# A diffusion-transformer layer on one core: the first feed-forward's way down by half products, and two conditioning vectors computed elsewhere

## The chip, the cores and the metric

The kernel runs on 1 core of one Trainium2 chip. The metric is the time of one execution on the device in microseconds (us). Three runs of the kernel before took 2833.11, 2833.44 and 2836.21 us; the median is 2833.44 us.

The engines are called as in the profile: PE (TensorE, matmuls), PEld (its weight loads), DVE (VectorE), ACT (ScalarE), POOL (GpSimd) and SP (SyncE, which issues the DMAs here). SBUF is the on-chip working memory, PSUM the memory into which PE writes.

## The reference, cut to what matters

One layer with two groups of tokens, 1024 latent and 128 context tokens, which the kernel handles together as T = 1152 columns (D = 1024 features, D_FF = 2816):

```python
def swiglu(h, w1, w3, w2):
    return (jax.nn.silu(h @ w1) * (h @ w3)) @ w2

def trunk_layer(x, mod, cache, lb, norm_g, ffn1, ffn2, mixer_w):
    m = [mod[:, i][:, None, :] for i in range(N_MOD)]
    x = x + 0.5 * m[2] * swiglu(modulate(x, norm_g[0], m[0], m[1]), *ffn1)
    mix, ctx = token_mixer(modulate(x, norm_g[1], m[3], m[4]), cache, lb, *mixer_w)
    x = x + m[5] * mix
    x = x + 0.5 * m[8] * swiglu(modulate(x, norm_g[2], m[6], m[7]), *ffn2)
    return x, ctx
...
        mod_p = (jax.nn.silu(c_ctx) @ w_ada[l] + b_ada[l]).reshape(1, N_MOD, D_MODEL)
        mod_s = (jax.nn.silu(c) @ w_ada[l] + b_ada[l]).reshape(c.shape[0], N_MOD, D_MODEL)
```

The "way up" of a feed-forward is `silu(h @ w1) * (h @ w3)`, its "way down" the product with `w2` (2816 x 1024) and the addition to x. The nine conditioning vectors `m[0]` to `m[8]` are rows of a matrix product of SiLU(c) (latent) and SiLU(c_ctx) (context) with `w_ada`; vectors 6 and 7 are first needed in the second feed-forward's norm.

## The kernel before, in words

Features lie on the 128 partitions, tokens along the free axis. Features come in 8 tiles (KT), hidden rows of a feed-forward in 22 tiles (NF), called rows 0 to 21 here. Each float32 product is made of three matmuls of a high and a low part: `wh*xh`, `wh*xl`, `wl*xh` (`mm3`, L535 to L542). The split into parts takes a copy on ACT and a subtraction on DVE or POOL.

The stages in order: first feed-forward up and down, mixer projections with the recurrence (`hgrn`), attention (`attn`, `heads`), merge, second feed-forward up and down, final norm. `ffn_fast` (L2181) runs a feed-forward; `l` is 0 for the first, 1 for the second.

**Half products.** A product of 2 x 2 blocks can be had with seven block products instead of eight, if sums of the blocks are formed before and after. `PRODUCTS` lists the order of the seven. The way up uses this in both feed-forwards (`fast_block`, L1882) after four (l = 0) or three (l = 1) plain rows: per row 7 products x 2 pairs of token quarters x 4 feature tiles x 3 matmuls of 288 columns = 168. Weights are made up to six products ahead by `fast_ops`: POOL forms sums (L1872), ACT the high part (L1876), DVE the low part (L1877).

**The second way down** uses it too. Pairs of rows 3 to 18 are taken in three groups of 2, 3 and 3 pairs (`GROUPS`). During the way up, `pair_sums` (L1933; DVE, L1939 to L1942) makes sums of the hidden rows and stores them in DRAM (`xd`), and `pair_weights` (L1948; POOL, L1965 to L1968) makes sums of quarters of `w2` and stores them (`wsum`). Then `down_sweep` (L2074) takes, per group and per pair of output tiles, seven products of 288 columns; `down_ops` supplies the split weights, `down_xs` the split hidden sums, and DVE adds to x (L2090). The remaining rows go plainly (`down_group`, `down_last`).

**The first way down** goes plainly, all of it: nine groups of two rows (`down_group`) and a last one of four (`down_last`), each over 8 output tiles and 3 chunks of 384 columns, with DVE adding each result to x (L569).

**Conditioning vectors.** Vectors 0 and 1 are made at the start by PE. The rest are made on DVE by `ada_sum` (L362): a transposed tile of `w_ada` times a broadcast row, 512 columns, with a running sum (L393), 32 such operations a vector, as two halves x 8 tiles x 2 rows. Vectors 2 to 5 are made in the first way up, 6 and 7 in the first way down (`self.bg`; one step after every third block of PE's work), 8 in the second way up. Their loads (256 KB each) go by SP's queue into two half tiles in turn; each load waits until DVE is done with the half tile.

**Order of the work.** A scheduler orders the instructions of each engine ahead of time, by the order in which the program emits them and by when their data and buffers should be ready; each engine then runs its list in order. The program weaves side work in by hand: generators (`ada`, `sums`, `xg`, `pre`, ...) advance by `next` at fixed points of the main loops. Large tiles (27 of them, tag `T`, `self.tt`) and smaller ones are shared by all stages. In `hgrn` a head has three chunks; PE's products of the scan stand among projection matmuls (`work`), which fill PE while DVE, POOL and ACT work on the chain of a chunk. In `heads` a head has two blocks of 9 key tiles; row maxima of the next block (`rowmax`: PE L1549, DVE L1550, two PSUM tiles), queries, keys and values of the next heads run beside.

Of the kernel before, what the change touches and what calls it, by code (L numbers as in the profile page):

```python
# [19 lines left out]
P = 128  # L20
# [13 lines left out]
H = 8  # L34
# [11 lines left out]
GROUPS = (3, 2), (7, 3), (13, 3)  # L46
# [47 lines left out]
class Trunk:  # L94
# [3 lines left out]
    def run(self):  # L98
        self.part, self.mode, self.chunks, self.bg = {}, "ffn1", ORDER, iter(())
        nc, tc, a = self.nc, self.tc, self.a  # L100
        with ExitStack() as st:
# [5 lines left out]
            self.xs = self.dp.tile([KT, P, T], F32, name="xs")  # L107
            self.modt = self.cp.tile([P, 9, KT, 2], F32, name="modt")
# [253 lines left out]
    def ada_sum(self, ms, cb, w2, small):  # L362
# [14 lines left out]
        for n, (h, i, k) in enumerate(units):  # L377
            if not i and not k:
                cs = [cb() if cb else self.half("cb")[:, :HD] for _ in range(2)]
                row = [self.half("row")[:, :HD] for _ in range(2)] if cb else cs  # L380
                for s in range(2):
                    nc.sync.dma_start(row[s], a["cr"][s : s + 1, ts(h, HD)].to_broadcast([P, HD]))
                if not n:
                    load(0)
                for s in range(2):
                    nc.scalar.activation(cs[s], row[s], AF.Silu)
                yield
# [14 lines left out]
            yield  # L402

# [452 lines left out]
    def hgrn(self):  # L856
# [77 lines left out]
        for p in range(H * NCH + 1):  # L934
# [31 lines left out]
        for i, _ in enumerate(work):  # L966
            if i % 2 == 0 and todo:
# [3 lines left out]
        for n, _ in enumerate(self.proj_gate(19, 3, pairs[3])):  # L971
            if n == 0:
                self.group()

# [266 lines left out]
    def heads(self, qn, ck, ckc, KT_, ktc, rope, w0, sums):  # L1241
# [37 lines left out]
        self.pend, self.mo = [], [None] * 8  # L1279
        pre = self.preload()  # L1280
        for h in range(H):
# [8 lines left out]
            for j in range(2):  # L1290
                rm = rowmax(h, 1) if not j else iter(()) if last else rowmax(h + 1, 0)
                sd = weave(side[j])
                for t, _ in enumerate(self.block(h, j, Q[h % 2], kset(h), vset(h))):
                    next(rm, None)
                    if t in SIDE:
# [3 lines left out]
                for _ in chain(rm, sd):  # L1299
                    pass  # L1300
        for _ in pre:
# [646 lines left out]
    def pair_weights(self, w2):  # L1948

        nc, pin = self.nc, self.tc.keep_in_program_order  # L1950
        self.wsum = self.dp.tile([sum(n for _, n in GROUPS), P, KT // 2, 4, P], F32, name="wsum")
        n = sum(n for _, n in GROUPS)
        for j in range(n):
            f = GROUPS[0][0] + 2 * j
            for m in range(KT // 2 if j < n - GROUPS[-1][1] else 1):
# [18 lines left out]
    def down_ops(self, w2):  # L1974

        nc = self.nc
        units = [(j, n, m) for j, n in enumerate(n for _, n in GROUPS) for m in range(KT // 2)]
# [5 lines left out]
        def load(u, key):  # L1983
# [3 lines left out]
            j, f = sum(v for _, v in GROUPS[:g]), GROUPS[g][0]  # L1987
            own = g == len(GROUPS) - 1 and m > 0
# [28 lines left out]
        for u, (g, n, m) in enumerate(units):  # L2017
            load(u + 1, 6)
            load(u + 1, 2)
            if g == len(GROUPS) - 1 and m:  # L2020
# [26 lines left out]
    def down_xs(self, g, X):  # L2047

        nc = self.nc
        j0 = sum(n for _, n in GROUPS[:g])  # L2050
        units = [(i, k) for i in PRODUCTS for k in range(GROUPS[g][1])]
# [22 lines left out]
    def down_sweep(self, g, m, X, ops, made, gm, S, after):  # L2074

        nc = self.nc
        n = GROUPS[g][1]
        first, last = g == 0, g == len(GROUPS) - 1
# [45 lines left out]
    def down_fast(self, w2, X, xg, ops, made, load_x, load_h, split_h, gm, nxt):  # L2124

        S = [self.tt(F32, "su")[:, :T].rearrange("p (m n) -> p m n", m=4) for _ in range(2)]
        rest = [2, *range(PLAIN[1] + 16, NF)]
        pend, ws = [], []
        self.folds = []
        for g, (f, n) in enumerate(GROUPS):  # L2130
            new = {} if g else X
            last = g == len(GROUPS) - 1
# [48 lines left out]
    def ffn_fast(self, l, gm, nxt):  # L2181
# [5 lines left out]
        self.puts, self.ticks, self.roles = [], 0, {}  # L2187
# [39 lines left out]
        spare = partial(self.tt, F32R) if l == 0 else partial(self.wide, dt=F32R)  # L2227
# [6 lines left out]
        def load_h(f):  # L2234
            if l and f < 2:
# [8 lines left out]
        def split_h(f, raw):  # L2244
            new = partial(self.tt, F32R) if f in (16, 17) and not l else split
# [11 lines left out]
        def load_w2(f):  # L2257
            return self.load_w(w2[f], 1, D, home=spare if f % 2 else None)

        sums = self.pair_weights(w2) if l else iter(())  # L2260
        dops, dmade, X = (self.down_ops(w2) if l else None), [], {}
        xg = self.down_xs(0, X) if l else None
        for f in range(plain, NF):
# [3 lines left out]
            for n in range(7):  # L2267
# [14 lines left out]
                if f == NF - 1 and l:  # L2282
# [4 lines left out]
                    for _ in range(GROUPS[0][1]):  # L2287
# [3 lines left out]
                    for k in ((0, 4), (), (), (), (1, 5), (2, 6), (3, 7))[n]:  # L2291
                        self.x[k] = self.tt(F32, f"x{k}")
                        if k % 4 < 3:
                            nc.sync.dma_start(self.x[k][:, :T], self.xs[k])
                elif f == NF - 1:
                    if n == 2:
                        raws = [load_h(0), load_h(1)]
                    elif n == 3:
                        ws.append(load_w2(0))
                        pend.append(split_h(*raws[0]))  # L2300
                    elif n == 4:
                        pend.append(split_h(*raws[1]))
                    elif n == 5:
                        ws.append(load_w2(1))
                        self.x = [load_x(0), load_x(1)]
# [3 lines left out]
        if not l:  # L2309
            self.x += [load_x(k) for k in range(2, KT)]  # L2310
        if l == 0:
            self.mixer_consts()
            self.bg = self.ada_sum((6, 7), lambda: self.bank("up", "cb", D // 2), partial(self.tt, F32), self.slim)
        if l:
            self.down_fast(w2, X, xg, dops, dmade, load_x, load_h, split_h, gm, nxt)
            return
        for f in range(2, NF):
            pend.append(split_h(*load_h(f)))
            if f % 2 and f < NF - 1:
                fs, hs = zip(*pend[:2])  # L2320
                self.down_group(w2, fs, hs, gm, ws or [load_w2(v) for v in fs])
                pend, ws = pend[2:], None
        for _ in self.bg:
            pass
        fs, hs = zip(*pend)
# [124 lines left out]
```

## Time and profile before

| | us |
|---|---|
| median of three runs | 2833.44 |
| the profiled execution, whole | 2831.82 |
| its span (first to last instruction) | 2830.0 |
| mean granted TensorE clock | 0.995 of full |
| PE idle in the recurrence (818 to 1420) | 17.0 |
| PE idle in attention's heads (1540 to 1860) | 10.1 |
| DVE busy in the first way down (534 to 818) | 215.97 |

Times of lines are from the start of the span. A line of a group of instructions reads: line, engine, operation, out<-in by the program's names, out<-in (partitions x elements, type), count | busy time, mean ns of one | idle time of the engine just before them and what ended most of it. A line by stage reads: from:to, length, then for each engine its busy time and in brackets the count of its instructions, the granted clock, the mean busy share of the 16 DMA engines and the GB/s that they moved. PE's matmuls are pipelined, so one lasts longer than the step from one start to the next.

### The profile page before, as it was taken

The page shows a single profiled execution, that of the slowest core. Times are in us where ns is not written, and L with a number is a line of the kernel's source. Part 1 is how long each engine was busy: PE and PEld are TensorE (multiplying, and loading weights), DVE is VectorE, ACT ScalarE, POOL GpSimd, SP SyncE. Part 2 cuts the span into 40 slices and gives each one's busy share as a digit, 9 for nine tenths or more (in the row PEclk, how much of TensorE's full clock was granted, in tenths as well). Part 3 has the DMA queues.
Part 4 walks back from the last instruction along what each step waited for, and adds up shares of the span by engine and source line. Part 5 has one row for each costly group of instructions (what it writes and reads, how often), then busy time and mean ns, then how long its engine had stood idle before and what let it go on. Part 6 is the DMA issues. An engine that isn't in the chain of part 4 may idle for free. (4 is left out here: it accounts for less than half of the span.)

```text
span 2830.0 us, 55726 instructions
## 1 busy us (share of the span) xinstructions
PE 2763.6 (98%) x21222; PEld 2633.5 (93%) x21222; DVE 2037.8 (72%) x4464; ACT 1302.9 (46%) x2696; POOL 926.4 (33%) x980
## 2 busy tenths in 40 slices
PE   8999999999999999999999999999999999999998
PEld 7999999999999998889998778689999999999997
DVE  7867777677678787877356777766766765568875
ACT  6533332321176676666436777741552322234332
POOL 0233232444222222222244444420414443423451
PEclk9999999999999999999999999999999999999999
DMA  6743443753121111112512001263454444358521
GB/s 261 228 130 118 130 125 118 260 180 117 57 82 57 45 63 38 66 41 84 192 60 98 19 15 30 84 232 104 154 171 130 145 156 134 116 164 253 164 85 67
DMA packets 219578, 337.64 MB, mean 119 GB/s; under 512 B 23664, under 2 KB 141360, under 8 KB 219312
## 3 DMA queue, kind: packets, MB, share of 16 engines
q1 hardware_dynamic: 219312, 334.10, 36.0%
q8 instruction: 167, 2.74, 0.4%
q14 instruction: 99, 0.81, 0.1%
HBM read 248.47 MB, written 85.54 MB: 118 GB/s over the span
## 5 line engine op out<-in xcount | busy, mean ns | idle before, releaser
L1902 PE MATMUL b<-xo,wo 128*128 128x288 f32 x3552 | 482.9, 295 | 0.0
L1902 PEld LDWEIGHTS b<-xo,wo 128*128 128x128 f32 x3552 | 474.8, 188 | 0.0
L1902 PE MATMUL b<-bh,wo 128*128 128x288 f32 x1776 | 366.0, 295 | 0.0
L539 PE MATMUL mm<-xh,wh 128*128 128x384 f32 x936 | 327.2, 350 | 5.5 <-DVE q L767 4.3
L541 PE MATMUL mm<-xh,wl 128*128 128x384 f32 x936 | 317.2, 339 | 0.0
L540 PE MATMUL mm<-xl,wh 128*128 128x384 f32 x936 | 316.6, 338 | 0.0
L1902 PEld LDWEIGHTS b<-bh,wo 128*128 128x128 f32 x1776 | 288.7, 188 | 0.0
L569 DVE SCALAR_TENSOR_TENSOR x<-dn,modt,x 128x256 f32<-128x256 f32 (+4 forms) x472 | 225.6, 499 | 83.8 <-PE dn L541 81.8
L1902 PE MATMUL b<-bl,wo 128*128 128x288 f32 x888 | 261.7, 295 | 0.0
L1876 ACT CAST wo<-raw 128x512 fp32r<-128x512 f32 x185 | 114.8, 621 | 221.1 <-issue 88.1
L539 PEld LDWEIGHTS mm<-xh,wh 128*128 128x128 f32 x936 | 176.4, 188 | 12.9 <-DVE q L767 5.5
L2103 PE MATMUL d<-xd,wd 128*128 128x288 f32 x1344 | 181.7, 297 | 5.0 <-DVE x L2090 3.0
L2103 PEld LDWEIGHTS d<-xd,wd 128*128 128x128 f32 x1344 | 180.0, 190 | 6.5 <-issue 4.4
L1877 DVE TENSOR_TENSOR wo<-raw,wo 128x512 fp32r<-128x512 f32 x185 | 127.4, 689 | 79.1 <-ACT wo L1876 76.5
L540 PEld LDWEIGHTS mm<-xl,wh 128*128 128x128 f32 x936 | 176.7, 189 | 0.9
L541 PEld LDWEIGHTS mm<-xh,wl 128*128 128x128 f32 x936 | 177.0, 189 | 0.0
L1599 POOL TENSOR_TENSOR ehl<-e,ehl 128x512 fp32r<-128x512 f32 x93 | 123.9, 1337 | 154.6 <-ACT ehl L1597 83.6
L393 DVE SCALAR_TENSOR_TENSOR junk<-wada,cb 128x512 bf16<-128x512 f32 x224 | 163.9, 732 | 5.5 <-DMA wada<-in_w_aT 4.6
L1902 PEld LDWEIGHTS b<-bl,wo 128*128 128x128 f32 x888 | 167.5, 189 | 0.0
L1872 POOL TENSOR_TENSOR ws<-raw 128x256 f32<-128x256 f32 x74 | 64.5, 892 | 283.1 <-DMA raw<-in_w 254.3
L539 PE MATMUL ps<-bh,wh 128*128 128x288 f32 (+1 forms) x448 | 135.7, 303 | 3.2 <-ACT bh L532 1.9
L1877 DVE TENSOR_TENSOR wo<-ws,wo 128x512 fp32r<-128x512 f32 x74 | 69.6, 940 | 92.4 <-ACT wo L1876 91.9
(477 smaller groups left out, 7163.9 us busy)
## 6 DMA issues: line engine op xcount, KB each, us to landing
raw<-in_w SPq DMA_DIRECT2D x148, 256.0 KB, 3.5
wada<-in_w_aT SPq DMA_DIRECT2D x112, 256.0 KB, 3.1
raw<-in_w SPq DMA_DIRECT2D x42, 512.0 KB, 3.8
raw<-in_w_in SPq DMA_DIRECT2D x41, 512.0 KB, 3.5
xr<-xd SPq DMA_DIRECT2D x56, 288.0 KB, 3.8
hr<-hs SPq DMA_DIRECT2D x26, 576.0 KB, 5.7
hb<-hd SPq DMA_DIRECT2D x44, 288.0 KB, 3.8
hs<-et SPq DMA_DIRECT2D x84, 144.0 KB, 2.3
```

What stands on the lines that cost most here:

```text
L393: nc.vector.scalar_tensor_tensor(junk, ws[n % 2], 1.0, cs[s], ALU.mult, ALU.mult, accum_out=o)
L539: pin(nc.tensor.matmul(ps, wh, xh, start=start and i == 0, stop=False))
L540: pin(nc.tensor.matmul(ps, wh, xl, start=False, stop=False))
L541: self.last_mm = nc.tensor.matmul(ps, wl, xh, start=False, stop=stop and i == n - 1)
L569: nc.vector.scalar_tensor_tensor(self.x[m][:, a:b], ps[:, a - lo : b - lo], self.modt[:, gm, m, s : s + 1], self.x[m][:, a:b], ALU.mult, A ...
L1599: eng.tensor_sub(el, e, eh)
L1872: nc.gpsimd.tensor_tensor(o[:, c], x[:, c], y[:, c], op)
L1876: nc.scalar.copy(wh, src[i])
L1877: nc.vector.tensor_sub(wl, src[i], wh)
L1902: nc.tensor.matmul(ps, w[:, k], x[:, k, :QW], start=first, stop=last, skip_group_check=home != i)
L2103: nc.tensor.matmul(ps, w[:, k], xv, start=start, stop=stop, skip_group_check=home != i)
```

## The change

- The first way down goes by half products too, by the code of the second: pairs of rows 4 to 19 in groups of 2, 3 and 3. `GROUPS` has an entry for each feed-forward, and `self.groups` takes its place in the functions. Rows 0 to 3, 20 and 21 stay plain (0 and 1 as one group, the other four in `down_last`). `pair_sums`, `pair_weights` and the first steps of `down_ops` and `down_xs` now run in the first way up too.
- The background sum of vectors 6 and 7 in the first way down is gone. A new function `ada_late` makes one vector by the same 32 operations. Vector 6 is made in `hgrn` from the last head's first chunk on, one operation at each slot; vector 7 in `heads`, three operations per block.
- `ada_late` loads the rows SiLU(c), SiLU(c_ctx) from DRAM (`crow`), where `ada_sum` stores them in the first way up.
- `mixer_consts` and the loads of x stand where the second feed-forward has its own.

```diff
-GROUPS = (3, 2), (7, 3), (13, 3)
+GROUPS = ((4, 2), (8, 3), (14, 3)), ((3, 2), (7, 3), (13, 3))
...
+                    if self.mode == "ffn1":
+                        nc.sync.dma_start(self.crow[h, s : s + 1], cs[s][0:1])
...
+    def ada_late(self, m):
...
+        wt = self.tt(F32, "wada")
+        ws = [wt[:, ts(v, HD)] for v in range(2)]
+        cs = []
+        for h in range(2):
+            t = self.tt(F32, "cb")
+            cs.append([t[:, ts(s, HD)] for s in range(2)])
+            for s in range(2):
+                nc.sync.dma_start(cs[h][s], self.crow[h, s : s + 1].to_broadcast([P, HD]))
...
+        for n, (h, k) in enumerate(units):
+            if n + 1 < len(units):
+                load(n + 1)
+            for s in range(2):
+                o = acc[:, h, k, s : s + 1]
+                self.tc.keep_in_program_order(
+                    nc.vector.scalar_tensor_tensor(junk, ws[n % 2], 1.0, cs[h][s], ALU.mult, ALU.mult, accum_out=o)
+                )
+                yield
...
+            if p == H * NCH - 3:
+                ada = self.ada_late(6)
...
                     next(work, None)
                     next(pre, None)
+                    if p > H * NCH - 4:
+                        next(ada, None)
...
+        ada = self.ada_late(7)
...
                     next(rm, None)
+                    if t % 3 == 1:
+                        next(ada, None)
...
-        rest = [2, *range(PLAIN[1] + 16, NF)]
+        plain = self.groups[0][0]
+        rest = [*range(2, plain), *range(plain + 16, NF)]
...
-        if l:
-            self.xd = self.dp.tile([sum(n for _, n in GROUPS), P, 7, 2, QW], F32, name="xd")
-            self.roles = {f + v: (j, v % 2) for j, f in enumerate(range(GROUPS[0][0], PLAIN[1] + 16, 2)) for v in range(2)}
+        self.xd = self.dp.tile([sum(n for _, n in self.groups), P, 7, 2, QW], F32, name=f"xd{l}")
+        self.roles = {f + v: (j, v % 2) for j, f in enumerate(range(plain, plain + 16, 2)) for v in range(2)}
...
-        sums = self.pair_weights(w2) if l else iter(())
-        dops, dmade, X = (self.down_ops(w2) if l else None), [], {}
-        xg = self.down_xs(0, X) if l else None
+        sums = self.pair_weights(w2)
+        dops, dmade, X = self.down_ops(w2), [], {}
+        xg = self.down_xs(0, X)
...
-            self.bg = self.ada_sum((6, 7), lambda: self.bank("up", "cb", D // 2), partial(self.tt, F32), self.slim)
-        if l:
-            self.down_fast(w2, X, xg, dops, dmade, load_x, load_h, split_h, gm, nxt)
-            return
-        for f in range(2, NF):
-            pend.append(split_h(*load_h(f)))
-            if f % 2 and f < NF - 1:
-                fs, hs = zip(*pend[:2])
-                self.down_group(w2, fs, hs, gm, ws or [load_w2(v) for v in fs])
-                pend, ws = pend[2:], None
-        for _ in self.bg:
-            pass
-        fs, hs = zip(*pend)
-        self.down_last(w2, fs, hs, gm, nxt)
+        self.down_fast(w2, X, xg, dops, dmade, load_x, load_h, split_h, gm, nxt)
```

More of the change, by code (lines that the diff above doesn't have):

```diff
@@ L1986, in load @@
             g, n, m = units[u]
-            j, f = sum(v for _, v in GROUPS[:g]), GROUPS[g][0]
-            own = g == len(GROUPS) - 1 and m > 0
+            j, f = sum(v for _, v in self.groups[:g]), self.groups[g][0]
+            own = g == len(self.groups) - 1 and m > 0
             part = lambda t, h: t[:, : h * n * P].rearrange("p (h k d) -> p h k d", h=h, k=n)
@@ L2049, in down_xs @@
         nc = self.nc
[L2050 to L2051 removed]
+        j0 = sum(n for _, n in self.groups[:g])
+        units = [(i, k) for i in PRODUCTS for k in range(self.groups[g][1])]
         raws = []
@@ L2244, in split_h @@
         def split_h(f, raw):
-            new = partial(self.tt, F32R) if f in (16, 17) and not l else split
+            new = partial(self.tt, F32R) if f < 2 else split
             hh, hl = new(name="hh")[:, :T], new(name="hl")[:, :T]
```

67 lines of the change are left out of this document (36 added, 31 removed).

## The prediction, made before the changed kernel ran

> **What bounds the kernel now.** I read the page first, then the busy times by stage, then single tiles for the spacing of the matmuls, then the groups of DVE and POOL in the stages that the change touches.
>
> ```profile
> span 2830.0 us, 55726 instructions
> PE 2763.6 (98%) x21222; PEld 2633.5 (93%) x21222; DVE 2037.8 (72%) x4464; ACT 1302.9 (46%) x2696; POOL 926.4 (33%) x980
> ```
>
> TensorE is busy all along, so a stage is as long as its matmuls need, plus what they wait. The stages, with the count of instructions behind each engine's busy time:
>
> ```profile
> core 0: us, PE busy (x) PEld busy (x) DVE busy (x) ACT busy (x) POOL busy (x), PEclk, DMA share, GB/s
> 133.00:534.00 401.00, 401.00 (x3026) 401.00 (x3025) 289.33 (x646) 126.12 (x245) 128.38 (x145) 1.00 0.41 132
> ...
> 2133.00:2551.40 418.40, 418.40 (x3157) 418.40 (x3156) 268.91 (x532) 126.27 (x256) 163.73 (x238) 1.00 0.44 142
> 2551.40:2738.00 186.60, 181.60 (x1347) 180.08 (x1347) 158.23 (x306) 77.67 (x150) 78.94 (x50) 0.99 0.57 177
> ```
>
> They are the first way up by half products, the second way up, and the second way down, which already runs by half products (the first, plain, follows below). Matmuls overlap, so the mean of one (about 0.3 us) is no price; the spacing is. Both ways up have PE without a gap: 401.00 / 3026 = 0.1325 us for a 288-column matmul. The second way down needs 186.60 / 1347 = 0.1385 us for the same form, so 0.006 x 1347 = 8.1 us of it are lost.
>
> For the plain way down, its first matmul, the first of the stage behind it, and two matmuls that stand 56 apart in the timeline:
>
> ```profile
> L539 PE MATMUL dn<-hh,wh x360: 279/338/692, 534.2 to 2817.8; 128*128 128x384 f32 x156, 128*128 128x512 f32 x12, 128*128 128x256 f32 x12
> ```
> ```profile
> L539 PE MATMUL mm<-xh,fh x24: 332/338/525, 814.8 to 854.9; 128*128 128x384 f32 x24
> ```
> ```profile
> 559.75 0.34 PE L540 MATMUL dn<-hl,wxh 128*128 128x384 f32 x1
> 569.52 0.34 PE L539 MATMUL dn<-hh,wh 128*128 128x384 f32 x1
> ```
>
> The stage takes 814.8 - 534.2 = 280.6 us. Its spacing is 9.77 / 56 = 0.1745 us for 384 columns. By the code it has 22 rows x 8 outputs x 3 chunks x 3 products = 1584 matmuls, 276.4 us; 4.2 us are waits and the norm's own matmuls.
>
> **The change, part by part.**
>
> *The first way down.* Eight pairs of rows (4 to 19) go by seven products instead of eight: 8 x 4 x 7 x 2 x 3 = 1344 matmuls of 288 columns. Rows 0 to 3, 20 and 21 stay plain: 6 x 8 x 3 x 3 = 432 of 384. Without stalls that is 1344 x 0.1325 + 432 x 0.1745 + 4.2 = 257.7 us, 22.9 less. But the same code in the second way down did not run at 0.1325. What held it there:
>
> ```profile
> L2103 PE MATMUL d<-xd,wd 128*128 128x288 f32 x1344 | 181.7, 297 | 5.0 <-DVE x L2090 3.0
> ```
> ```profile
> 2670.00:2690.00 20.00, 18.01 (x125) 17.80 (x124) 19.31 (x38) 7.42 (x15) 13.31 (x10) 0.91 0.56 167
> ```
>
> PE waited 5.0 us there, mostly for DVE, which is busy for 158.23 of 186.60 us (85%). The worst wait, 2.0 us near 2678, is followed by a lower granted clock (0.91 over 20 us, so 0.09 x 20 = 1.8 us more). Splits, product counts, group sizes (2, 3, 3) and transfers of the new stage are those of this one, and the two moved vectors no longer run in it. So I take 0.1385: 186.1 + 75.4 + 4.2 = 265.7 us, **14.9 less**. Bounds: 22.9 less, and 0 if DVE holds it for as long as it lasts now.
>
> The Trainium skill ("TensorE: Matmul & The Clock Gate", Part 1) has the clock halve only after an idle window of about 3.4 us and asks for no gap over about 3 us. By that a 2.0 us wait would cost itself alone, and the gain would be 16.7; the row differs, and I keep the row.
>
> *The first way up gets the sums.* It keeps its 128 conditioning products and gains the pair sums, the quarter and weight sums and the first splits for the way down. From the second way up, where such sums stand now (DVE, then POOL), and the first way up as it is (DVE, then POOL):
>
> ```profile
> L1942 DVE TENSOR_TENSOR hp<-et 128x288 f32<-128x288 f32 x16 | 7.3, 454 | 0.3
> ...
> L2068 DVE TENSOR_TENSOR xd<-xr,xd 128x576 fp32r<-128x576 f32 x6 | 7.0, 1174 | 3.7 <-ACT xd L2067 3.7
> ```
> ```profile
> L1872 POOL TENSOR_TENSOR raw<-raw,ws 128x256 f32<-128x256 f32 x36 | 25.8, 737 | 81.7 <-DVE wo L1877 58.8 <-issue 22.8
> L1966 POOL TENSOR_TENSOR wq<-wq 128x128 f32<-128x128 f32 x22 | 14.9, 679 | 1.2
> ...
> L1968 POOL TENSOR_TENSOR wq<-wq 128x128 f32<-128x128 f32 x22 | 11.2, 509 | 0.0
> ```
> ```profile
> L393 DVE SCALAR_TENSOR_TENSOR junk<-wada,cb 128x512 bf16<-128x512 f32 x128 | 95.8, 748 | 3.0 <-DMA wada<-in_w_aT 2.3
> L1877 DVE TENSOR_TENSOR wo<-raw,wo 128x512 fp32r<-128x512 f32 x89 | 61.0, 686 | 41.6 <-ACT wo L1876 40.3
> L1877 DVE TENSOR_TENSOR wo<-ws,wo 128x512 fp32r<-128x512 f32 x36 | 34.0, 945 | 37.8 <-ACT wo L1876 37.3
> ...
> L1906 DVE TENSOR_TENSOR et<-b,et 128x288 f32<-128x288 f32 x36 | 16.4, 457 | 9.1 <-PE b L1902 9.1
> ```
> ```profile
> L1872 POOL TENSOR_TENSOR ws<-ws,raw 128x256 f32<-128x256 f32 x36 | 32.8, 931 | 0.0
> ```
>
> DVE: four groups of pair sums like the one shown, 4 x 7.3, and 7.0 for the splits are 36 us more, 289.3 + 36 = 325 of 401 us (81%). POOL: four groups on quarters of weights, from 14.9 down to 11.2, about 52 us more, 180 (45%). At 72% (now) and 64% (second way up) of DVE, PE lost nothing; at 85%, in the second way down, 8.1 of 186.6 us (4.3%). So the bounds are 0 and 4.3% x 401 = 17 us. I take **1 us**, near the two ways up: weights are split up to six ahead of their use and each is good for 24 matmuls (6 x 24 x 0.1325 = 19 us), in the way down for only 12 or 18. A gain I exclude, since PE has no gap to close.
>
> *Vector 6 at the recurrence's end.* Thirty-two products of the kind that run in the first way down now, and DVE there from the last head's first chunk (the copy at 1309.75) on:
>
> ```profile
> L393 DVE SCALAR_TENSOR_TENSOR junk<-wada,cb 128x512 bf16<-128x512 f32 x64 | 43.4, 677 | 1.0 <-DMA wada<-in_w_aT 1.0
> ...
> L393 DVE DVE_READ_ACCUMULATOR junk<-wada,cb 128x1 f32 x64 | 5.3, 82 | 0.0
> ```
> ```profile
> 1309.75 0.42 DVE L1075 COPY_PREDICATED A<-mask,lv 128x96 f32<-128x96 uint8 x2
> ```
> ```profile
> 1300.00:1325.00 25.00, 25.00 (x301) 23.54 (x301) 24.27 (x51) 12.78 (x33) 9.06 (x11) 1.00 0.20 70
> 1325.00:1350.00 25.00, 25.00 (x359) 23.28 (x358) 13.11 (x40) 14.36 (x43) 4.53 (x7) 1.00 0.29 101
> 1350.00:1375.00 25.00, 25.00 (x237) 23.68 (x236) 8.40 (x19) 10.51 (x25) 3.19 (x5) 1.00 0.41 140
> 1375.00:1400.00 25.00, 25.00 (x169) 23.56 (x167) 6.50 (x15) 12.69 (x19) 3.21 (x2) 1.00 0.79 287
> ```
>
> One costs (43.4 + 5.3) / 64 = 0.76 us, 32 cost 24 us, and DVE has 12 + 17 + 18 us free after 1325. Only the first eight, 6 us, fall where it is full. Bounds 0 and 6; I take **1**, as PE has gate matmuls in store there (25.00 of 25.00 busy). Behind each waiting load in SP's queue stand the gates' stores and the weights for the next stage:
>
> ```profile
> SPq L374 <- DVE junk L393: 229.6, 81, 5.9
> ```
>
> SP waited 2.8 us on average for such a load, 5.9 at most. Those stores and loads have 25 us and more until their use, so I price this at nothing; without that cover it would be 16 x 2.8 = 45 us on SP, some of it late weights at 1400. A vector also brings 16 loads and four broadcasts of 256 KB, 5 MB, into a DMA share of 0.20 to 0.41; at the 287 GB/s of the last row that is 18 us of transfer, over more than 50 us. Taking 64 products out of the way down (49 us of DVE) brings nothing by itself, as PE lost at most 4.2 us there.
>
> *Vector 7 in attention*, three products per block, so in the first eleven of 16 blocks. A block takes 320 / 16 = 20 us. Blocks with queries and row maxima (the first half of a head) and without alternate:
>
> ```profile
> 1540.00:1860.00 320.00, 309.92 (x1451) 243.12 (x1449) 235.91 (x437) 245.96 (x466) 147.78 (x120) 1.00 0.13 37
> ```
> ```profile
> 1620.00:1640.00 20.00, 19.94 (x95) 16.11 (x94) 16.66 (x32) 14.81 (x28) 11.55 (x10) 1.00 0.03 7
> 1640.00:1660.00 20.00, 19.94 (x97) 15.81 (x96) 13.69 (x28) 16.58 (x35) 8.38 (x7) 1.00 0.10 26
> ...
> 1800.00:1820.00 20.00, 17.82 (x83) 13.42 (x83) 19.08 (x37) 14.08 (x28) 10.24 (x8) 1.00 0.15 41
> ```
>
> Three products add 2.3 to 2.5 us (0.677 or 0.748, and 0.08 for the sum's read): 16.6 becomes 19.1 of 20 in five such halves (heads 1 to 5), 13.7 becomes 16.2 in the others. The one stretch that has 19.08 now shows PE idle for 2.18 us instead of 0.06. So the upper bound is 5 x 2.1 = 11 us, the lower 0. I take **5**, since the stretch at 1800 also brings in the next stage's tiles. Here PE waits behind row maxima: DVE frees the two PSUM tiles that PE's next row-maximum matmul needs, and everything behind it on PE waits too. On SP the weights of the next heads stand behind the vector's loads, but those come 7 us apart and find their half tile free; of the 27 large tiles 25 are held by then, so the second pair of broadcasts waits until the first pair's tile is free, once, within the bounds above.
>
> The four small stores of the conditioning rows are nothing beside 334 MB. **Sum:** -14.9 + 1 + 1 + 5 = **-7.9 us**. The profiled execution took 2831.82 us (span 2830.0), 1.6 under the median of 2833.44. From the median: **2825.5 us**.
>
> **The rivals.**
>
> *A: attention takes back what the way down gives.* For it: 19.1 of 20 us on DVE, a level at which PE loses 2 us per 20. Against: the other half of each head can absorb. At 11 us the sum is -1.9: 2831.5 us, no change.
>
> *B: DVE and POOL hold up the first way up, and the kernel gets slower.* Operations with both inputs in SBUF wait for POOL: the split behind a POOL sum takes 945 ns, the one without 686, while one that reads PSUM (457) does not differ. Busy time that needs this path would be 325 - 5 x 16.4 (five groups that read PSUM) = 243 on DVE plus 180 on POOL, 423 of 401 us; about 9 us on DVE (36 x 0.26) and some 14 on POOL (two groups, 36 x (931 - 737) ns each) are waiting counted as work, so 400: just full, where it is 289 - 82 + 128 - 23 = 312 now. In-order queues do not fill it without gaps. If it decides, the stage grows by 17 (the bound above) to 23 us, say 20: -14.9 + 20 + 1 + 5 = +11: 2844.5 us. It makes the kernel slower by over 0.2% from 15 us on. The Trainium skill ("SBUF — State Buffer", SBUF: two separate sides) calls the shared port pair an exclusive lock that blocks the loser for the whole instruction. The trace agrees by 945 against 686.
>
> *C: no stalls in the way down*, as they hang on a few collisions (5.0 us of waits): -22.9 + 7 = -15.9: 2817.5 us.
>
> *D: fewer matmuls, but not sooner.* The second way down moves the most of the stages above, 177 GB/s at a DMA share of 0.57. If the new stage waits for its transfers as much as it has fewer columns to do, the gain is gone: -14.9 + 14.9 + 7 = +7: 2840.5 us. Against: the waits of the second way down are put down to DVE, not to a DMA.
>
> **How the numbers follow.** Forecast 0.50, A 0.20, B 0.15, C 0.10, D 0.05. A measurement tells about 0.2%, 5.7 us. The forecast's own range is 2819 to 2831, of which some four fifths lie under 2827.8; with C that makes faster 0.53. A and the rest of the forecast make no change 0.29; B and half of D, slower 0.18. The range runs from 2815 (C with small stalls) to 2846 (B).
>
> **What would show it.** PE without a gap from 133 to 534 with DVE near 325 us; 1344 matmuls on the first way down's tiles at 0.138 us, the stage some 15 us shorter; PE busy 25.00 in each 25 us from 1300 to 1400; attention up to 5 us longer with PE waiting for row maxima. It is wrong if the first way up has PE waiting for split weights or PSUM tiles, or if attention grows by over 10 us, or if the way down stays over 275 us.

## The result and the profile after

The changed kernel takes 2880.97 us (median of 4 runs, 2877.97 to 2884.28) beside 2833.28 us of the kernel before (4 runs); the ratio is 1.0167, with an interval of [1.0152, 1.0183]. It is slower by 48 us, where 8 us less were forecast. The profiled execution took 2883.85 us. First the page of after, then its stages; the columns are those of the stage table in the prediction.

```profile
span 2882.0 us, 57099 instructions
PE 2770.9 (96%) x21414; PEld 2629.6 (91%) x21414; DVE 2112.3 (73%) x4587; ACT 1333.5 (46%) x2816; POOL 973.6 (34%) x1089
```
```profile
133.80:563.40 429.60, 412.28 (x3027) 408.53 (x3026) 313.95 (x717) 118.57 (x255) 180.91 (x238) 0.98 0.54 169
563.40:754.20 190.80, 182.44 (x1345) 178.94 (x1345) 161.89 (x314) 77.47 (x152) 77.83 (x51) 1.00 0.56 177
754.20:831.60 77.40, 77.40 (x438) 76.56 (x438) 51.45 (x105) 33.14 (x62) 23.55 (x16) 1.00 0.29 101
831.60:1454.10 622.50, 598.33 (x6568) 558.50 (x6567) 488.38 (x1231) 394.02 (x949) 152.34 (x230) 0.99 0.24 81
...
1560.90:1911.70 350.80, 328.71 (x1466) 256.96 (x1466) 264.73 (x507) 249.09 (x471) 151.82 (x121) 0.96 0.17 51
```

They are the first way up, the first way down by half products, its plain rest, the recurrence, and attention's heads. The same stages of before, but for the way up (401.00 us, in the prediction):

```profile
534.20:814.80 280.60, 279.30 (x1590) 277.63 (x1589) 212.57 (x498) 72.30 (x102) 107.83 (x49) 1.00 0.41 142
814.80:1430.20 615.40, 598.37 (x6568) 559.36 (x6567) 463.76 (x1165) 393.40 (x949) 151.52 (x230) 0.99 0.22 73
...
1536.90:1860.60 323.70, 313.62 (x1468) 245.91 (x1467) 237.93 (x440) 248.79 (x471) 149.38 (x121) 1.00 0.13 39
```

| stage | before | after | difference | forecast |
|---|---|---|---|---|
| first way up | 401.0 | 429.6 | +28.6 | +1 (0 to 17) |
| first way down | 280.6 | 268.2 | -12.4 | -14.9 |
| recurrence | 615.4 | 622.5 | +7.1 | +1 (0 to 6) |
| heads | 323.7 | 350.8 | +27.1 | +5 (0 to 11) |

These make +50.4 of the 52.0 us between the two profiled executions. The way down brought what it should; three stages that only took over side work gave it back five times.

**First way up.** PE idled 429.60 - 412.28 = 17.3 us; of the other 11 us, some 9 are the lower granted clock (0.02 x 429.6). DVE is busy for 314 of 430 us (73%), so it isn't full. Its waits tell more. The row answers to the L393 row of before, where 3.0 us stood in the last column (line numbers move between the kernels: L1925 and L1927 below are L1872 of before). Then come SP's longest waits in this stage, each with its total, its count and the longest one:

```profile
L396 DVE SCALAR_TENSOR_TENSOR junk<-wada,cb 128x512 bf16<-128x512 f32 x128 | 94.1, 735 | 41.0 <-DMA wada<-in_w_aT 40.6
```
```profile
SPq L2023 <- POOL wq L2020: 67.8, 18, 8.3
SPq L1907 <- DVE wo L1930: 57.7, 24, 5.3
SPq L1843 <- DVE et L1994: 49.3, 15, 5.6
```

One such place, as SP, DVE and PE saw it (start, duration, and in brackets the wait before):

```profile
321.45 0.33 SPq L2023 DMA_DIRECT2D wsum<-wq  x1
321.88 1.40 SPq L375 DMA_DIRECT2D wada<-in_w_aT  x1
323.37 0.38 SPq L2024 DMA_DIRECT2D wsum<-wq  x1
323.85 0.37 SPq L375 DMA_DIRECT2D wada<-in_w_aT  x1
```
```profile
325.95 0.69 DVE L396 SCALAR_TENSOR_TENSOR junk<-wada,cb 128x512 bf16<-128x512 f32 x1 [4.84 <-DMA wada<-in_w_aT]
326.57 0.08 DVE L396 DVE_READ_ACCUMULATOR junk<-wada,cb 128x1 f32 x1
326.57 0.45 DVE L1963 TENSOR_TENSOR et<-b,et 128x288 f32<-128x288 f32 x1
```
```profile
327.08 0.61 PE L1955 MATMUL b<-bh,wo 128*128 128x288 f32 x1 [3.80 <-DVE et L1963]
```

SP had issued nothing since 312.77: it waited 8.3 us at the store of a quarter sum (L2023), until POOL had made that sum. A conditioning load stands behind this store in SP's queue. Its product stands at the head of DVE's queue and waits 4.84 us for it. Behind the product stands the addition that frees a PSUM tile, and PE waits 3.80 us for that.

**Heads.** Vector 7's products did not run three to a block. SP's queue shows the broadcast rows loaded at once, and the vector's first weights 200 us later; the stretches of 20 us show what followed:

```profile
1560.67 0.80 SPq L420 DMA_DIRECT2D cb<-crow  x2
...
1761.42 0.81 SPq L425 DMA_DIRECT2D wada<-in_w_aT  x2
```
```profile
1741.00:1761.00 20.00, 19.96 (x97) 15.73 (x97) 15.79 (x31) 16.31 (x32) 8.88 (x8) 1.00 0.03 7
...
1781.00:1801.00 20.00, 12.74 (x38) 10.18 (x37) 18.55 (x44) 4.60 (x9) 4.75 (x4) 0.71 0.34 112
```

All 32 products run from 1764 to 1817 us, nearly every second operation of DVE there (32 of 68), and PE falls to 12.74 of 20 us at a clock of 0.71. The vector wants 28 large tiles with what attention holds (25, and one for weights and two for rows); there are 27. The weights' tile was given the place of a key tile (the low half of the first), whose last reader is a score matmul of head 4.

### The profile page after: what moved, and what is told of

Its sections match the earlier page's. It is cut to its first block, busy times and chain, and to the rows that moved or that the text cites. A ratio compares the mean times of both kernels' runs of the same rounds, so it can differ in the third digit from the quotient of the medians.

```text
span 2882.0 us, 57099 instructions
## 1 busy us (share of the span) xinstructions
PE 2770.9 (96%) x21414; PEld 2629.6 (91%) x21414; DVE 2112.3 (73%) x4587; ACT 1333.5 (46%) x2816; POOL 973.6 (34%) x1089
## 5 line engine op out<-in xcount | busy, mean ns | idle before, releaser
L1955 PE MATMUL b<-bh,wo 128*128 128x288 f32 x1776 | 375.5, 300 | 16.6 <-DVE et L1963 11.7
L2156 PE MATMUL d<-xd,wd 128*128 128x288 f32 x2688 | 364.7, 297 | 13.2 <-DVE x L2143 8.5
L2156 PEld LDWEIGHTS d<-xd,wd 128*128 128x128 f32 x2688 | 359.3, 189 | 18.4 <-ACT wd L2094 6.2
L579 PE MATMUL mm<-xh,wh 128*128 128x384 f32 x936 | 327.1, 350 | 10.5 <-DVE sg L881 4.7
L1955 PEld LDWEIGHTS b<-bh,wo 128*128 128x128 f32 x1776 | 294.9, 192 | 20.1 <-DVE et L1963 12.5
L2121 POOL TENSOR_TENSOR xd<-xr,xd 128x576 fp32r<-128x576 f32 x70 | 111.9, 1617 | 179.4 <-ACT xd L2120 177.8
L1929 ACT CAST wo<-ws 128x512 fp32r<-128x512 f32 x74 | 45.7, 618 | 244.2 <-POOL ws L1925 224.1
L2143 DVE SCALAR_TENSOR_TENSOR x<-d,modt,x 128x288 f32<-128x288 f32 (+2 forms) x324 | 137.7, 462 | 23.6 <-PE d L2156 20.8
L396 DVE SCALAR_TENSOR_TENSOR junk<-wada,cb 128x512 bf16<-128x512 f32 x160 | 118.9, 743 | 43.1 <-DMA wada<-in_w_aT 42.6
```

The source lines that it names most:

```text
L396: nc.vector.scalar_tensor_tensor(junk, ws[n % 2], 1.0, cs[s], ALU.mult, ALU.mult, accum_out=o)
L579: pin(nc.tensor.matmul(ps, wh, xh, start=start and i == 0, stop=False))
L1929: nc.scalar.copy(wh, src[i])
L1955: nc.tensor.matmul(ps, w[:, k], x[:, k, :QW], start=first, stop=last, skip_group_check=home != i)
L2121: (nc.vector if k == 1 else nc.gpsimd).tensor_sub(lo, raw, hi)
L2143: nc.vector.scalar_tensor_tensor(xv, src[:, v], self.modt[:, gm, mi, s : s + 1], xv, ALU.mult, ALU.add)
```

## The experiments

Theory: (1) in the first way up, loads stand late in SP's in-order queue behind stores that wait for other engines, and the operations that wait for these loads hold up DVE's and POOL's in-order queues; (2) in attention, the missing tile bunches the products; (3) in the recurrence, either of the two. The main rival is time: DVE, POOL and their shared path simply have too much to do. All stage lengths below are from first matmul to first matmul; a stage whose code is the same in two runs differs by up to 4.4 us (the first way up 427.3 to 431.7; the recurrence, unchanged in twelve of them, 619.1 to 621.5, beside 622.5 in after). The first way down, whose own work none of the experiments changes, takes 262.9 to 270.3 us. e1 to e13 are one execution each, so stage lengths are compared, not totals. e1, e6 and e13 leave out most loads of the vectors' weights, so they compute other vectors; they show times only.

### e1 and e2: the conditioning loads

e1, then e2 (`nw` is the count of half tiles, four):

```diff
-            if n + 1 < len(units):
+            if n + 1 < (len(units) if len(ms) == 1 else 2):
```
```diff
-        w2 = w2("wada")
-        ws = [w2[:, :HD], w2[:, HD : 2 * HD]]
+        tiles = [w2("wada") for _ in range(2 if len(ms) == 4 else 1)]
+        ws = [t[:, ts(v, HD)] for t in tiles for v in range(2)]
...
-            if n + 1 < len(units):
-                load(n + 1)
+            if n + nw - 1 < len(units):
+                load(n + nw - 1)
```

> The first way up alone is changed: the conditioning weights of vectors 2 to 5 are loaded for the first two of their 64 units only, and all 128 products read these two (the product is another one; the DVE work is the same, 128 of 0.74 us). Theory (late loads): the products hold up DVE because their loads stand late in SP's queue, not because DVE or the path it shares with POOL is full. Then DVE's 40.6 us behind these loads go, PE's stalls of 2 to 4 us with them, and the stage comes down from 429.5 to 401 to 410 us. Rival (full path): DVE and POOL still have the same 313.6 and about 180 us of work to bring together; the stage stays at 422 or more. In between, 410 to 422, both would have a part. The other stages stay.

> The first way up alone is changed: the conditioning weights of vectors 2 to 5 lie in four half tiles (one more large tile, 25 of 27 become 26 of 27) and are loaded three units ahead of their product instead of one; the same loads and the same products. Theory (late loads): a load that SP issues up to 5 us late now still lands in time; DVE's 40.6 us behind them fall below 10, the stage from 429.5 to 403 to 412 us. Rival (full path): the stage stays at 422 or more, as the work on DVE and POOL is the same. A second rival is that SP's queue delays the weights of the way up as well (raw tiles, 57.7 us of SP waiting there): then the stage comes down by half at most, to 412 to 420.

e1: 409.9 us, at the edge of the theory's range. e2: 416.4 us, the range of its second rival; DVE's wait for the weights is 1.2 us. The loads are 20 of the 28.6 us. What is left in e1 comes once in two rows, and POOL shows it:

```profile
330.49 0.46 POOL L2018 TENSOR_TENSOR wq<-wq 128x128 f32<-128x128 f32 x1 [11.62 <-DMA wq<-in_w]
...
332.29 1.44 POOL L1925 TENSOR_TENSOR ws<-raw 128x256 f32<-128x256 f32 x2
```

POOL waits 11.62 us for the loads of a quarter sum, and the way up's own weight sums (L1925) stand behind it. The loads were issued from 325.31 us on, right behind the store of the last pair sum (324.32), whose kind of tile they need: there are three of these narrow tiles, and the loads of a unit (one set of quarter sums) take two.

### e5 and e6: the pair sum in a tile of its own

```diff
-        u = self.fp.tile([P, CW], F32, tag="hf", bufs=self.hfb, name="hp")[:, :QW]
+        u = self.slim("hp")
```

> The loads of e2 (three units ahead), and the last pair sum no longer in one of the three narrow tiles that the quarter sums use for their loads, but in a tile of another kind that is free there. Theory (two queues, one cause): what e1 and e2 left, stalls of 1.5 to 2.4 us once in every pair of rows (46 us), comes from POOL: the quarter sum stands in POOL's queue for a load that waits for that narrow tile, and the way up's own weight sums stand behind it. Then the stage falls from e2's 416.4 to 403 to 410 us. Rival (the path that DVE and POOL share): the stalls stay where they are, 414 or more.

> The loads of e1 (two units' weights only, so the products are others) and the pair sum in a tile of its own as in e5. Theory: both causes are gone, all of the DVE and POOL work is still there, and the stage takes 401 to 404 us, as before the change. Rival (shared path): e1's 409.9 us stay, 408 or more.

e6 takes 404.7 us with DVE and POOL at least as busy as in after (321 and 190 us), so the path that they share isn't what holds it. But e5, with the loads back, takes 429.5, a miss. Its waits of POOL and of SP:

```profile
POOL ws L1927 <- DMA raw<-in_w: 145.4, 15, 14.4
```
```profile
SPq L2028 <- POOL wq L2025: 123.8, 23, 9.6
```

Now the way up's own weights are late, behind quarter-sum stores. A wait taken off one load had gone to another in the same queue.

### e9 and e10: the stores issued by POOL

```diff
-                nc.sync.dma_start(self.wsum[j][:, m, 0:2], a[:, P:].rearrange("p (k d) -> p k d", k=2))
+                nc.gpsimd.dma_start(self.wsum[j][:, m, 0:2], a[:, P:].rearrange("p (k d) -> p k d", k=2))
```

> From the changed kernel, one edit: the 46 stores of the quarter sums are issued from POOL's own queue, right behind the sums, and no longer from SP's, where they waited 67.8 us in 18 waits for POOL; nothing else is moved. Theory (one SP queue in order): every load behind such a store comes sooner, the conditioning weights among them; DVE's 40.6 us behind these fall below 20, and the first way up from 429.5 to 408 to 420 us. Rival: SP's other waits (57.7 us for DVE's splits, 49.3 for the pair sums) hold the loads as long, or POOL loses what SP gains because each store now takes time in its queue; 425 or more.

> e5 (conditioning weights three units ahead, the last pair sum in a tile of its own) with the quarter sums' stores issued from POOL as in e9. Theory: e5 took 429.5 us because SP then stood 123.8 us in waits for the quarter sums, so that the way up's own weights came late (POOL idle 145.4 us behind them); with these stores off SP the loads ahead and the own tile bring what they did in e6, 402 to 410 us. Rival: the waits go over to the pair sums' stores, which still stand in SP's queue; 415 or more.

e9: 421.9 us, a fourth of the loss back; DVE's wait for its weights falls to 23.5 us, not below 20. e10: 437.1, a miss. The stores leave SP's queue but not its loads: SP now waits 117.4 us in 21 waits (up to 9.4) at loads whose narrow tile is still being stored, 16.9 in 13 (up to 2.4) in e5. In e5 it had stood 123.8 us at the stores themselves; the wait went from the store to the load behind it.

### e12: the same queue, in another order

`store()` issues the stores of the unit before, in this order; the loads of this unit stand two steps ahead of it.

```diff
-        self.nt, self.hfb = (("hf", 3), 3) if self.mode == "ffn1" else (("sl", 4), 3)
+        self.nt, self.hfb = (("hf", 5), 5) if self.mode == "ffn1" else (("sl", 4), 3)
...
                 yield
                 yield
+                store()
                 pin(nc.gpsimd.tensor_tensor(s1, a21, a22, ALU.add))
```

> e5 (conditioning weights three units ahead, the last pair sum in a tile of its own) with five narrow tiles in place of three, and each quarter sum's stores held back in SP's queue until the next unit's loads have been issued, so that SP finds the sum done. All loads, stores, products and sums of the changed kernel are there. Theory (SP's in-order queue): e9 and e10 only moved the waits; here SP waits neither for POOL's sums nor for a narrow tile to be stored, its waits for both fall from 123.8 and 16.9 us in e5 to below 30 in all, and the first way up takes 403 to 412 us. Rival (traffic, or the path of DVE and POOL): e6 was fast because 62 loads of 256 KB were missing, not because none was late; with all the traffic and all the work the stage stays at 417 or more.

413.7 us with all the loads, stores and sums: under the rival's 417, 1.7 over the theory's range. SP's waits for the sums are gone from its list. Its worst stall (PE 3.9 us at 385) had POOL wait 10.76 us for weights whose load was issued at 375.46, behind six stores of pair sums (366.29 to 372.00) and a conditioning load (374.04).

### e3, e7, e8, e11: vector 7

e3 (the second pair of rows is loaded when the first is used up), and what e7 adds:

```diff
-            t = self.tt(F32, "cb")
+            t = t if h and one else self.tt(F32, "cb")
```
```diff
-                    if t % 3 == 1:
+                    if j and t % 3 != 1:
                         next(ada, None)
```

e8 makes both vectors at the recurrence's end with one set of rows; e11 makes vector 7 between recurrence and heads.

> Attention alone is changed: vector 7's two pairs of broadcast rows share one large tile, the second pair being loaded when the first half of the products is done, so that 27 large tiles are wanted and not 28. Theory (tile shortage): the load tile no longer waits for a key tile to come free, and the 32 products run three to a block from the first head on, not all within 1764 to 1817 us; the stage of the heads comes down from 350.9 to 325 to 335 us (before: 323.7). Rival (DVE's time): 24 us more on an engine that is busy for 74% cost about as much wherever they stand; 342 or more.

> Attention alone is changed, from e3: six products in each block without queries, none in those with queries, in place of three in each. Theory (the full half): e3's 13.8 us over the stage before come from the blocks with queries, where DVE is busy for 18 to 19 of 20 us; the other half can take 4.6 us more (13.7 becomes 18.3), so the stage of the heads falls from 337.5 to 324 to 331 us. Rival (row maxima): any product ahead of a row maximum makes PE wait for it, in either half; 335 to 341.

> Vector 7 leaves attention: both vectors' products go through the recurrence's end with one set of broadcast rows, from one chunk later on, two products per slot and three in the closing loops. Attention has no conditioning product. Theory: the stage of the heads is back at 323.7 us (322.5 to 325), so all of its 27.2 us are vector 7's; the recurrence pays for 16 more loads in SP's queue and 24 us more of DVE, with 60 us of DVE free there: 620 to 628 us. Rival: the extra time in attention has another source, such as the tiles of the next stage that come later; then the heads keep 8 us or more of it.

> Vector 7 alone is moved, from the heads to the stage between recurrence and heads (106.7 us, DVE busy for about half, SP nearly idle), with one tile for its broadcast rows and two to three products between that stage's steps. Theory (place): the heads are back at 323.7 us (322.5 to 326) and the stage ahead of them grows by 0 to 6 us, as DVE has 50 us free there for 24 us of products and no store waits ahead of the loads; together 430.4 to 436 us instead of 457.6. Rival (conditioning products hold up DVE's in-order queue wherever they stand): together 442 or more, as in the heads with the light half (440.9).

e3: 337.5 us, between both ranges. The products are spread, and half of the loss is gone; 13.8 us stay. e7: 334.7, so the half matters little. e8: the heads are back at 323.8, so the 27 us are vector 7's alone, but the recurrence takes 637.7, beyond the forecast; PE's longest wait there is 8.1 us, near 1431, for weights whose load came late (ACT waits 8.4 us for it). e11: heads 323.5, the stage before them 117.5 (106.7): 441.0 together, just under the rival's 442 and far above the theory. Thirteen of attention's 27 us were the bunching; the other 11 to 14 are the price of 32 products in the three places tried (e3, e7, e11). In the heads PE then waits most for row maxima (9.3 us in e3, 5.9 in e7, 2.1 in before), in e11 for the squares of a norm (3.9 us beside 1.3); how the products bring about the latter was not followed up.

### e4 and e13: vector 6

e4 (with two products per slot), then e13:

```diff
-            if p == H * NCH - 3:
+            if p == H * NCH - 1:
                 ada = self.ada_late(6)
```
```diff
-            if n + 1 < len(units):
+            if n + 1 < (2 if m == 6 else len(units)):
                 load(n + 1)
```

> The recurrence's end alone is changed: vector 6 starts two chunks later, after DVE's full stretch (19.3 of 20 us), with two products per slot in place of one. Theory (place): the stalls at 1312 (2.1 us) and 1337 us (1.8 us), which the first products caused, go; the stage comes down from 622.5 to 617 to 619.5 us (before: 615.4). Rival (queue): the vector's loads on SP hold up stores and weights of the gates wherever it stands; the stage stays at 621 to 625, with the stall of 1.6 us at 1428 or a longer one.

> The recurrence's end alone is changed: vector 6's weights are loaded for the first two of its 16 units only, and all 32 products read these two (the product is another one; DVE's work is the same). Theory (queue): the 4 to 7 us that the recurrence grew by come from the loads in SP's queue, behind which the gates' stores and weights stand; without them it takes 615.5 to 617.5 us. Rival (DVE): they come from the products, the first of which fall into DVE's full stretch; 619.5 to 622.5 us, with the stalls of about 2 us near 1312 and 1337.

e4: 620.2 us, what unchanged code takes. The stalls near 1312 and 1337 are gone or halved, but two stand behind late loads in their place (PE 2.4 us near 1440, 1.0 near 1410). e13: 618.9; without the loads those two stay (2.1 us at 1315, 1.7 at 1340). So both have a part: the first products, in DVE's full stretch, and the loads (in after, 1.6 us near 1428 and 1.2 near 1445, gone in e13); moving the vector trades one for the other. That is read from the stalls: the length of e13's stage lies between the two forecasts and only 0.2 us under the shortest unchanged one.

### e14, e15, e16: together

e14 is e12 and e7, with the pair sums stored at the fourth product of a row, kept in this order. e15 has the second edit (and no vector in attention), e16 the same with vectors 6 and 7.

```diff
-                for t in self.puts:
-                    self.put(*t)
-                self.puts = []
+                if l or n == 3:
+                    for t in self.puts:
+                        i = self.put(*t)
+                        if not l:
+                            self.tc.keep_in_program_order(i)
+                    self.puts = []
```
```diff
-        ada = self.ada_sum((8,) if l else (2, 3, 4, 5), None, partial(self.tt, F32), self.slim)
+        ada = self.ada_sum((8,) if l else (2, 3, 4, 5, 7), None, partial(self.tt, F32), self.slim)
```

> All that helped together: e12 in the first way up, there also the pair sums' stores held back to the middle of the next row, behind the next weights' loads (e12's worst stall, 3.9 us, had POOL wait 10.8 us for weights whose load stood behind these stores); vector 7 in the halves without queries, from one tile, as in e7. Theory (SP's in-order queue): the first way up falls from e12's 413.7 to 403 to 410 us, the heads take 334 to 336 us; in all 2881 less 20 to 26 less 16, 2839 to 2846 us, 1.002 to 1.005 of the time before. Rival (what e12 left is traffic or the shared path): the first way up stays at 412 to 416 us, in all 2848 to 2852 us.

> e14, with vector 7 no longer in attention but as a fifth vector of the first way up, which shares that stage's broadcast rows: 32 more products (24.6 us of DVE, 322.6 becomes 347 of 404 us) and 16 more loads there, five products per row slot in place of four. Theory (it is late loads, not DVE's time, that hold the way up): the way up grows from 403.9 by 0 to 6 us, the heads go back to 323.7; in all 4 to 10 us less than e14: 2822 to 2829 us, 0.996 to 0.999 of the time before. Rival (DVE's time): at 86% busy the way up loses what the second way down loses at 85%, 4.3% of it, 17 us; in all 2837 or more.

> e15, with vector 6 in the first way up as well: 372 of 404 us of DVE (92%), 32 more loads than in e14, and no conditioning product in recurrence or attention. Theory: the recurrence goes back to 615 to 616 us (5 less) and the heads stay at 323.7; the way up is DVE's limit now and grows by 6 to 14 us over e14's 403.9: 2821 to 2833 us in all. Rival (DVE's time): the way up grows by 20 us or more; 2838 or more in all.

The first way ups of e14, e15 and e16, and the recurrence and heads of e16:

```profile
134.20:538.10 403.90, 401.73 (x3026) 401.26 (x3025) 322.62 (x722) 120.12 (x253) 180.36 (x237) 1.00 0.58 182
```
```profile
133.50:553.30 419.80, 406.02 (x3027) 403.17 (x3025) 348.62 (x781) 116.48 (x250) 194.84 (x237) 1.00 0.57 182
```
```profile
133.00:574.40 441.40, 413.20 (x3026) 408.84 (x3024) 369.57 (x848) 116.80 (x251) 186.02 (x238) 0.98 0.58 183
843.20:1457.60 614.40, 595.87 (x6567) 556.19 (x6567) 463.10 (x1163) 392.46 (x948) 150.18 (x230) 0.99 0.22 74
1564.40:1887.60 323.20, 313.26 (x1467) 246.28 (x1466) 238.59 (x440) 248.62 (x471) 148.93 (x121) 1.00 0.13 39
```

e14's way up takes 403.9 us, with the DVE and POOL work of after, all its loads and stores, and more GB/s (182 beside 169): 2.9 over before. That settles (1): the order of SP's queue and the short lead of its loads, with the tiles that set both, cost 25.7 of the 28.6 us. In all, e14 takes 2832.66 us (10 runs), a ratio of 1.0005 [0.9995, 1.0014]: no change from before, and 48 us less than after (a little better than forecast). Its way down gives 15.5 us (265.1); the heads (+10.5), the recurrence (+5.7) and the way up (+2.9) take them, and later stages, whose code is not changed, came out 3.5 us shorter.

e15 and e16 met their rival: 2841.04 us, 1.0035 [1.0022, 1.0047], and 2853.47 us, 1.0075 [1.0062, 1.0089]. The heads and, in e16, the recurrence are back (323.2, 614.4), but the way up grows by 16 and 37.5 us. DVE waits for none of the added loads there, which speaks for DVE's time: 323 us of it go with 3 us lost in the way up, 349 with 19, 370 with 40, and in e16 POOL waits 56.0 us for DVE's splits (9.1 in e14). But the added loads also stand in SP's queue, where each waits until a product has freed its tile. The total of such waits, their count and the longest one, in e14 and then in e15 (e16: 133.9 us in 64):

```profile
SPq L376 <- DVE junk L398: 60.0, 35, 5.9
```
```profile
SPq L376 <- DVE junk L398: 128.3, 53, 6.7
```

Ahead of e15's longest stall (PE 3.32 us at 484.65) SP stood 10.7 us at three of them, from 461.9 to 473.3; the way up's own weights were issued behind them, at 475.03, and POOL waited 10.88 us for these. DVE itself was idle for 4.42 us just then, waiting for a split that needed them. So the queue has a part here too, and how much of the 16 and 37.5 us is DVE's time alone stays open. No version that was tried beats the kernel before.

## Why the prediction was wrong

- **First way down** (-14.9): right. Its matmuls came 190.80 / 1344 = 0.142 us apart, close to the 0.1385 taken from the second way down, and PE's waits are the same kind, mostly for DVE, but longer (8.4 us beside 5.0). The 2.5 us that it fell short lie within the differences between runs.
- **First way up** ("I take 1 us", bounds 0 and 17): the step that failed most. It added up busy time of DVE and POOL and left out SP, though the step moves 46 stores and 92 small loads into the queue in which 64 conditioning loads stand, each only one unit ahead of its product. The comparison with the second way up did not carry over: that one has a quarter of the conditioning products (32). The bound from "85% busy" bounded the wrong cause; the true one had no term. Rival B had the right place and nearly the right size (17 to 23) with another mechanism; e6 and e14 show that the shared path is not it, as the same work fits into 404 us. Two of the prediction's own signs of being wrong came true: PE waits for PSUM tiles in the way up (11.7 us for the additions on DVE, L1963, that free them), and attention grows by over 10 us.
- **Vector 7** ("I take 5", bounds 0 and 11): the count of large tiles was wrong by one. It had 25 held and the second pair of rows waiting once; the vector wants three tiles, and the one that waited was the weights', for 200 us, after which the products had no spacing left. Even spread as described (e3), the price is 13.8, over the bound: five halves at 2.1 us left out the other halves and the first block.
- **Vector 6** ("I take 1", bounds 0 and 6): 4 to 7 us, at its bound. Two steps failed: the products in DVE's full stretch did cost PE about 3 us (stalls of 2.1 and 1.7 us in e13, 0.8 us before), and the loads, priced at nothing for their cover of 25 us, brought stalls near 1428 and 1445 (gone in e13) and others where e4 moved them.
- The forecast gave SP's waits in the way up no term, and their total would have been no sign either way. In the way up of before it is longer than in after:

```profile
SPq L374 <- DVE junk L393: 144.8, 55, 5.1
SPq L1854 <- DVE wo L1877: 66.0, 33, 7.6
```

Those are loads that wait for their own tile, and PE had no gap there, so what stood behind them came in time. After, a store waits for POOL, POOL for DVE or for a load (71.9 and 69.3 us in this stage), and DVE for a load behind that store.

The chances held a slip as well: four fifths of 0.50 and the 0.10 of C make 0.50 for faster, not 0.53.

## What to carry to other kernels

When side work moves into another stage, write down that stage's DMA queue in its order, and ask of each load behind a waiting trigger how long before its use it is issued; busy shares of the engines don't show it. Count tiles by name at the place of use: one too many did not slow vector 7 a little here, it delayed its work by 200 us and then bunched it. Where a fix only moves a wait (e5, e10, e4), try the order of the queue next, as e12 and e14 did. Work that is added to an engine also adds loads that wait for it; test the two apart before the engine's time gets the blame.

## What the runs showed of the hardware

A PE wait of under 2 us can be enough for half the clock, and one of 3.6 us need not be. Over the 3.4 us after a wait of 2.48 us, and after the 3.80 us shown above, in the changed kernel:

```profile
277.00:280.40 3.40, 3.40 (x16) 3.40 (x17) 3.40 (x10) 0.00 (x0) 0.00 (x0) 0.56 0.45 151
327.10:330.50 3.40, 3.40 (x14) 3.40 (x15) 3.40 (x10) 0.00 (x0) 0.00 (x0) 0.50 0.45 146
```

In steps of half a us the first of these reads 0.50 from 277.5 to 280.5 and 1.00 from 281.0 on: the clock drops after PE has resumed (276.95), and stays down for some 3 us. After 2.12 us (494.7) it was 0.66. Shorter waits did it too: over the 3.4 us after one of 1.78 us in e8 (448.4) it was 0.72, after one of 1.89 us in e9 (458.3) 0.57. After 1.57 us (446.8) it stayed at 1.00, after 2.05 us in e14 (378.4) as well, and so it did after 2.95 us in e8 (277.6) and 3.59 us in e11 (326.4). The length of the wait alone does not tell. The Trainium skill ("TensorE: Matmul & The Clock Gate", Part 1) names one idle window of about 3.4 us; the traces show a loss after waits of about half that, and none after one of 3.59 us.

To issue one of the 46 stores takes 0.54 to 0.56 us of POOL's own time (medians in e10) and 0.33 us of SP's (e5). The stores land about as fast from either: the median from issue to landing of the DMAs on `wsum` is 2.8 us in e10 and 2.9 in e9, issued by POOL, and 2.3 in e5 and 3.4 in after, issued by SP.
